# Attention scores of two heads on their own rows, expert down products half by half, and the last norm's gain ahead of its root

## The chip, the core and the metric

The kernel runs on one NeuronCore of a Trainium2 chip. The metric is the device time of one execution in microseconds (us), and less is better. The core has TensorE (PE in the profile; PEld is its weight load), VectorE (DVE), ScalarE (ACT), GpSimd (POOL) and SyncE (SP), which issues the transfers.

## What is computed

The reference is a transformer in float32 for one sequence of 256 tokens of 1024 channels. First come two layers, each a gated feed-forward block, a mixer and a second feed-forward block. Then come a state-space and short-convolution layer, a mixture of 16 experts of which each token uses two, and a last norm.

A mixer has three kinds of attention side by side, and a projection joins them:

```python
o_a = mla_mixer(h_a, ...)    # 6 heads, keys of 96
o_b = nsa_mixer(h_b, ...)    # 6 heads of 64 in 2 key groups: compressed + selected + window
o_c = diff_mixer(h_c, ...)   # 4 heads, each the difference of two softmaxes, keys of 32
x = x + jnp.concatenate([o_a, o_b, o_c], axis=-1) @ w_out[l]
```

The experts and the end are

```python
for e in range(N_EXPERTS):
    h = jax.nn.silu(t @ w_gate[e]) * (t @ w_up[e])
    out = out + combine[:, e:e + 1] * (h @ w_down[e])
...
return rmsnorm_2(h, norm_final)[:, N_META:]
```

## The kernel before, in words

The program is written with tiles and pools. A scheduler puts the instructions of each engine in order by its own estimate of when each can run, with the order of the program as the first guide. `in_turns` issues a first product and binds the others to come after it. `behind` does the same for any instructions.

Large weights are loaded by SP into tiles `st` (four buffers), 1 MB each, and split into a high and a low part (`wh`, `wl`: ScalarE at L166, VectorE at L167), which enter as separate products.

TensorE's products all bear the line of the helper `mm` (L98), and many copies on ScalarE that of a helper too, so they are told apart by their tiles.

In a mixer the string `ORDER` (L40) gives the order of the steps. A `w` step is a group of input columns, `mp`, `np` and `dp` prepare the three kinds of attention, `m0` to `m5`, `n0` to `n5` and `d0` to `d3` are heads, and `df` ends the differential ones. PSUM has eight banks here: three with tag S (scores, and half of the output projection's results), two with T (transposes), one with O (outputs of a pair of heads) and two with W (input columns, the differential outputs `po`, and the other half of the projection). A bank is free for the next user when its last reader is done.

A head goes like this. `scores` (L744; `nsa_head` has its own for the compressed and selected branch) makes a bank S of scores for the second and first half of the queries against the keys, and adds the causal mask as a product with the identity. `softmax` takes maxima on VectorE (L725), exponentials with their sums on ScalarE (L729) and reciprocals on VectorE (L732). For the compressed branch it also clamps (L727, L731). The gates follow at L734. `scale_rows` scales the weights on POOL or VectorE (L739). Then come three transposes (`ptp`, L691), a copy to `PT` and the products with the values. These wait in a list until two heads are there, and `pv_pair` does both in turns, each into its own half of the partitions of one bank (`opair`). `store_o` splits the result into `oh` and `ol`.

An nsa query tile holds a head of key group 0 on rows 0 to 63 and a head of group 1 on rows 64 to 127. The keys `ks` and `kw` (L802, L803) are stored once for each group, with zeros in the other group's rows, so that a product over all 128 rows gives the scores of one head. The differential keys `kC` (L892) are stored four times in the same way, each with 32 rows filled by a copy at L905. POOL fills in the zeros (L804, L805, L894). Heads of a pair are `n0` and `n1`, `n2` and `n3`, `n4` and `n5`. With `divmod(h, 3)` the head's number gives the group and the query tile.

The output projection (from L973) loads four units of `w_out` with one transfer each and goes over the chunks of `oh` and `ol` in the order 0, 1, 3, 4, 5, 6, 7, 2. Its products run wherever TensorE has time.

The experts run in eight rounds of two experts with 64 slots each. A round makes gate and up products, their activation (L1786 to L1788), transposes (L1800, copied at L1802), the down products into two banks `y0` and `y1` for the halves of the channels (L1803 on), their scaled high and low parts `ys` (L1634, L1814), and, one round later, `add`, which sums them into four banks `acc[t][half]` for two token tiles and two halves. The weights come in pieces of 512 KB into a ring of 44 places. `finish` (L1818 on) takes sums of squares of the four banks, the inverse root (`moe_inv`, L1570 on), and multiplies by root and gain into `os`, which leaves in four transfers.

## Time and profile before

| | us |
|---|---|
| median of three runs (lowest, highest) | 1529.91 (1529.6, 1532.09) |
| the profiled execution | 1532.0 |
| its span, first to last instruction | 1529.8 |
| TensorE busy in the span | 1492.0 |
| VectorE busy | 1025.1 |
| ScalarE busy | 729.7 |

The mean granted TensorE clock was 0.994 of full speed. The profile is of one execution, and the durations in the text are from that one. A row of a timeline begins with the start in us from the span's beginning, then the length of the merged instructions, the engine, the line, the operation and what is written from what. Successive instructions of an engine overlap by some tens of nanoseconds, so that a length is a little more than an engine's step.

### The profile page before, as it was taken

Reading aid. Unit: us, or ns where it says so; the run is one execution under the profiler, and the core shown is the slowest. Engines: PE = TensorE matmul, PEld = TensorE weight load, DVE = VectorE, ACT = ScalarE, POOL = GpSimd, SP = SyncE. Lnnn points to the kernel's source line nnn. Section 1 sums busy time; section 2 is a strip of 40 time slices with the busy share of each in tenths; the row PEclk is TensorE's granted clock in tenths of the full one; section 3 lists DMA queues with packets and bytes.
Section 4 is the critical chain, followed back from the end, with each engine's and each line's share of the span. In section 5 each row is a group of like instructions: output and inputs, shape, how many; then the busy total and the mean of one; then the engine's idle time right before and its main releaser. Section 6 shows DMA issues by size and latency. Waiting matters only on the chain.

```text
span 1529.8 us, 25415 instructions
## 1 busy us (share of the span) xinstructions
PE 1492.0 (98%) x9970; PEld 1253.6 (82%) x9970; DVE 1025.1 (67%) x2013; ACT 729.7 (48%) x1382; POOL 91.4 (6%) x142
## 2 busy tenths in 40 slices
PE   8999999999999999999999999999899999999996
PEld 7999998788999989999888999999799987344432
DVE  6886775868677786778576877779988875122112
ACT  6555565755454555455665655547554442011011
POOL 0000000520000000000025000000510100000000
PEclk9999999999999999999999999999999999999999
DMA  7756664216555565655640555566533588999993
GB/s 252 246 175 193 189 164 145 78 56 205 186 188 193 167 193 192 193 192 164 169 130 2 193 185 176 192 192 207 153 123 116 189 296 336 359 393 393 393 394 117
DMA packets 223559, 308.93 MB, mean 202 GB/s; under 512 B 20908, under 2 KB 167608, under 8 KB 223432
## 3 DMA queue, kind: packets, MB, share of 16 engines
q1 hardware_dynamic: 223128, 306.71, 60.1%
q8 instruction: 80, 1.31, 0.4%
q10 hardware_dynamic: 304, 0.53, 0.1%
q14 instruction: 47, 0.39, 0.1%
HBM read 306.16 MB, written 1.05 MB: 201 GB/s over the span
## 4 chain that ended last, share of the span: by engine, by line
PE 92%; DVE 5%; ACT 1%; issue 1%; DMA 0%; POOL 0%; ACTq 0%; DVEq 0%
PE gu L98 32%; PE acc L98 16%; PE proj L98 6%; PE win L98 6%; PE gate L98 4%; PE y L98 4%; PE up L98 4%; PE h L98 3%; PE wo L98 3%; PE S L98 3%; PE moe L98 1%; PE opair L98 1%; PE ptp L691 1%; PE zp L98 1%; PE xgp L98 1%; DVE wl L167 1%
## 5 line engine op out<-in xcount | busy, mean ns | idle before, releaser
L167 DVE TENSOR_TENSOR wl<-st,wh 128x1024 fp32r<-128x1024 f32 (+1 forms) x370 | 447.5, 1220 | 198.9 <-ACT wh L166 187.7
L166 ACT ACTIVATE wh<-st 128x1024 fp32r<-128x1024 f32 (+1 forms) x382 | 399.3, 1059 | 336.5 <-PE gu L98 134.4
L98 PE MATMUL gu<-xhl,wh 128*128 128x512 f32 (+1 forms) x1440 | 487.8, 392 | 3.1 <-ACT wh L166 2.2
L98 PE MATMUL gu<-xhl,wl 128*128 128x256 f32 x1408 | 381.6, 280 | 0.0
L98 PEld LDWEIGHTS gu<-xhl,wh 128*128 128x128 f32 x1440 | 268.2, 190 | 61.0 <-ACT wh L166 2.6
L98 PEld LDWEIGHTS gu<-xhl,wl 128*128 128x128 f32 x1408 | 260.8, 189 | 0.3
L98 PE MATMUL acc<-hx,wh 128*128 128x256 f32 x1408 | 252.1, 281 | 0.0
L98 PEld LDWEIGHTS acc<-hx,wh 128*128 128x128 f32 x1408 | 216.3, 188 | 1.6
L98 PE MATMUL acc<-hx,wl 128*128 128x256 f32 x704 | 196.8, 281 | 0.0
L98 PE MATMUL proj<-uhl,wh 128*128 128x272 f32 (+2 forms) x592 | 127.6, 306 | 5.3 <-DVE dv L1184 1.6
L98 PEld LDWEIGHTS acc<-hx,wl 128*128 128x128 f32 x704 | 132.6, 188 | 0.0
L98 PE MATMUL win<-wh,xhl 128*128 128x256 f32 (+1 forms) x576 | 109.7, 286 | 0.2 <-DVE xT L410 0.2
L98 PEld LDWEIGHTS proj<-uhl,wh 128*128 128x128 f32 x592 | 95.9, 191 | 10.5 <-ACT cv L1222 2.8
L98 PE MATMUL proj<-uhl,wl 128*128 128x272 f32 (+2 forms) x328 | 95.0, 290 | 0.0
L98 PEld LDWEIGHTS win<-wh,xhl 128*128 128x128 f32 x576 | 90.8, 191 | 4.2 <-issue 3.4
L98 PE MATMUL win<-wl,xhl 128*128 128x256 f32 (+1 forms) x288 | 81.9, 284 | 0.0
L394 ACT ACTIVATE hx<-up 128x512 fp32r<-128x512 f32 x44 | 27.7, 630 | 87.8 <-DVE up L393 87.8
L98 PEld LDWEIGHTS proj<-uhl,wl 128*128 128x128 f32 x328 | 62.5, 191 | 0.2
L1814 DVE SCALAR_TENSOR_TENSOR ys<-y,rc,ys 128x512 fp32r<-128x512 f32 x16 | 11.7, 749 | 67.2 <-ACT ys L1634 66.8
L739 POOL TENSOR_SCALAR P<-P,mx 128x128 f32<-128x128 f32 (+2 forms) x88 | 53.2, 621 | 57.9 <-DVE mx L732 41.8
L729 ACT ACTIVATE P<-S,mx 128x256 f32<-128x256 f32 (+2 forms) x128 | 48.9, 394 | 13.4 <-DVE mx L725 3.6
L98 PEld LDWEIGHTS win<-wl,xhl 128*128 128x128 f32 x288 | 55.0, 191 | 0.3
(522 smaller groups left out, 2133.7 us busy)
## 6 DMA issues: line engine op xcount, KB each, us to landing
st<-ffn_wg SPq DMA_DIRECT2D x44, 1024.0 KB, 5.7
st<-ffn_wu SPq DMA_DIRECT2D x44, 1024.0 KB, 5.4
st<-ffn_wd SPq DMA_DIRECT2D x44, 1024.0 KB, 4.7
st<-w_in SPq DMA_DIRECT2D x36, 1024.0 KB, 5.4
st<-w_out SPq DMA_DIRECT2D x16, 1024.0 KB
mf<-expert_w_gate SPq DMA_DIRECT2D x25, 512.0 KB, 9.8
mf<-expert_w_down SPq DMA_DIRECT2D x21, 512.0 KB, 10.7
mf<-expert_w_up SPq DMA_DIRECT2D x18, 512.0 KB, 11.3
```

Source lines behind the costliest of these rows:

```text
L98: return self.nc.tensor.matmul(out, lhsT, rhs, start=start, stop=stop, skip_group_check=True)
L166: hi = self.nc.scalar.activation(hl[0], src, AF.Copy)
L167: sub = (self.nc.gpsimd if lo[i] == "p" else self.nc.vector).tensor_sub(hl[1], src, hl[0].bitcast(F32))
L394: nc.scalar.activation(hh, up, AF.Copy)
L691: tr(p[:, i * 128:(i + 1) * 128], b, ident)
L729: nc.scalar.activation(P[:, d], s[:, c], AF.Exp, bias=m[:, 0, i:i + 1], accum_out=m[:, 1, i:i + 1])
L739: (nc.gpsimd if key + str(i) in "c0 c1 c2 d0 d1 m0 w0 w1".split() else nc.vector).tensor_scalar(P[:, d], P[:, d], r[:, i:i + 1], None, op0 ...
L1814: V.scalar_tensor_tensor(yl, py[half], rc[:, 1:2], yh.bitcast(F32), op0=OP.mult, op1=OP.subtract)
```

## The change

The change has four parts.

1. Scores. `ks`, `kw` and `kC` are stored once, without zeros. The new `scores_pair`, and the same by hand in `nsa_pair`, computes two heads in turns, each with the rows of the query tile that are its own (64 for nsa, 32 for the differential heads) into a bank S of its own. The masks are added on all rows afterwards. `nsa_pair(hg)` takes the heads hg and 3 + hg of one query tile together, and `ORDER` names the pairs. MLA heads stay as they were.
2. Output weights. As the pairs are now other heads, their rows of `w_out` are loaded in another order, by four transfers a unit in place of one.
3. Experts. The down products finish the first half of the channels and then the second, where they alternated. `add` goes through the halves likewise.
4. Last norm. The gain is multiplied into the first halves before the root is known, and ScalarE then scales them in place. VectorE does the second halves in one step each. All four sums of squares are on ScalarE, where one was on VectorE.

```diff
@@ L40 @@
-ORDER = "w01 w5 w2 mp m0 m1 w8 w3 w4 w6 np w7 dp m2 m3 d0 d1 n0 n1 d2 d3 n2 n3 n4 n5 m4 df m5"
+ORDER = "w01 w5 w2 mp m0 m1 w8 w3 w4 w6 np w7 dp m2 m3 d0 d1 n0 d2 d3 n1 n2 m4 df m5"
...
+        def scores_pair(banks, q, k, rows):
+
+            in_turns([lambda s=s, r=r, c=c, t=t, n=n: self.mm(s[:, c], q[t][r], k[r, 0:n], t == 1, False)
+                      for t, c, n in ((1, C1, 256), (0, C0, 128)) for s, r in zip(banks, rows)])
+            for s in banks:
+                self.mm(s[:, 128:256], self.identb, self.maskb, False, False)
+                self.mm(s[:, C0], self.identb, self.maskb, False, True)
...
-            ks = ap.tile([128, 2, 16 + T], F32, name="ks", tag="hA")
-            kw = ap.tile([128, 2, T], F32, name="kw", tag="cqT")
-            nc.gpsimd.memset(ks, 0.0)
-            nc.gpsimd.memset(kw, 0.0)
+            ks = ap.tile([128, 16 + T], F32, name="ks", tag="hA")
+            kw = ap.tile([128, T], F32, name="kw", tag="cqT")
+            nc.gpsimd.memset(ks[:, 15:16], 0.0)
...
-            for g in range(2):
-                q = slice(g * 64, (g + 1) * 64)
-                nc.vector.tensor_copy(ks[q, g, 16:16 + T], p3[q, 0:256])
-                nc.vector.tensor_copy(kw[q, g], p3[q, 256:512])
+            nc.vector.tensor_copy(ks[:, 16:16 + T], p3[:, 0:256])
+            nc.vector.tensor_copy(kw, p3[:, 256:512])
...
-            for g in range(2):
-                ACT(ks[g * 64:(g + 1) * 64, g, 0:15], p[g * 64:(g + 1) * 64, 0:15], scale=0.5)
+            ACT(ks[:, 0:15], p[:, 0:15], scale=0.5)
...
-        def nsa_head(h):
...
-            s = self.bank("S", "S")
-            self.mm(s[:, 0:272], qt[1], ks[:, g], True, False)
-            self.mm(s[:, 0:16], im, self.cmask[:, 1], False, False)
-            self.mm(s[:, 144:272], im, mb, False, False)
-            self.mm(s[:, 272:416], qt[0], ks[:, g, 0:144], False, False)
-            self.mm(s[:, 272:288], im, self.cmask[:, 0], False, False)
-            self.mm(s[:, 288:416], im, mb, False, True)
...
-            s = self.bank("S", "S")
-            scores(s, qt, kw[:, g], kw[:, g, 0:128])
...
+        def nsa_pair(hg):
+
+            rows = [slice(64, 128), slice(0, 64)]
+
+            two = [self.bank("S", "S") for _ in range(2)]
+            in_turns([lambda s=s, r=r, t=t, c=c, n=n: self.mm(s[:, c:c + n], qt[t][r], ks[r, 0:n], t == 1, False)
+                      for t, c, n in ((1, 0, 272), (0, 272, 144)) for s, r in zip(two[::-1], rows)])
+            for s in two:
+                self.mm(s[:, 0:16], im, self.cmask[:, 1], False, False)
+                self.mm(s[:, 144:272], im, mb, False, False)
+                self.mm(s[:, 272:288], im, self.cmask[:, 0], False, False)
+                self.mm(s[:, 288:416], im, mb, False, True)
+            for g, s in enumerate(two):
+                h = 3 * g + hg
+                P = ap.tile([128, 416], F32, name="P", tag="P", bufs=6)
+                scale_rows(P, SEGC, softmax(s, P, SEGC, gt[:, h, 0:4], -1e29), "c")
+                p, pt, n = transposes(blocks(P), "ptp")
+                nc.scalar.copy(pt, p[:, 0:n])
+                p2 = self.bank("T", "ptc")
+                cpt = ap.tile([16, T], F32, name="cpt", tag="cpt", bufs=2)
+                for t in range(2):
+                    tr(p2[0:16, t * 128:(t + 1) * 128], P[:, 384 + t * 16:400 + t * 16], ident)
+                nc.vector.tensor_copy(cpt, p2[0:16, 0:T])
+                pv("s", pt, [hV[:, t, 128 + g * 64:192 + g * 64] for t in range(2)])
+                waiting.setdefault("c", []).append((cpt, vcmp[0:15, g * 64:(g + 1) * 64]))
+            o = self.bank("O", "opair")
+            pv_pair(o, "s", True, False)
+            c0, c1 = waiting.pop("c")
+            in_turns([lambda o_=o_, c=c: self.mm(o_, c[1], c[0][0:15], False, False)
+                      for o_, c in ((o[64:128, 0:256], c1), (o[0:64, 0:256], c0))])
+            two = [self.bank("S", "S") for _ in range(2)]
+            scores_pair(two[::-1], qt, kw, rows)
+            for g, s in enumerate(two):
+                P = ap.tile([128, 384], F32, name="P", tag="P", bufs=6)
+                scale_rows(P, SEGS, softmax(s, P, SEGS, gt[:, 3 * g + hg, 4:6]), "w")
+                p, pt, n = transposes(blocks(P), "ptp")
+                nc.vector.tensor_copy(pt, p[:, 0:n])
+                pv("w", pt, [hV[:, t, 256 + g * 64:320 + g * 64] for t in range(2)])
+            pv_pair(o, "w", False, True)
+            store_o(3 + hg, o[:, 0:256])
...
-            kC = [ap.tile([128, 4, T], F32, name="kC", tag=tag) for tag in ("kC0", "hC")]
-            for k in kC:
-                nc.gpsimd.memset(k, 0.0)
+            kC = ap.tile([128, 2, T], F32, name="kC", tag="kC0")
...
-            for c in range(2):
-                for i in range(4):
-                    q = slice(i * 32, (i + 1) * 32)
-                    (nc.vector.tensor_copy if i % 2 else nc.scalar.copy)(kC[c][q, i], p2[q, c * T:(c + 1) * T])
+            nc.vector.tensor_copy(kC, p2[:].rearrange("p (c t) -> p c t", c=2))
...
-            for j in range(2):
-                k = kC[c][:, 2 * (h % 2) + j]
-                s = self.bank("S", "S")
-                scores(s, halves(qC[:, c]), k, k[:, 0:128])
+            two = [self.bank("S", "S") for _ in range(2)]
+            r0 = h % 2 * 64
+            scores_pair(two[::-1], halves(qC[:, c]), kC[:, c], [slice(r0 + 32, r0 + 64), slice(r0, r0 + 32)])
+            for s in two:
...
-        wo = [self.cols(a["w_out"][l], (b * 256, b * 256 + 256)) for b in range(4)]
+
+        def wo_unit(b):
+
+            st = self.wp.tile([128, 2048], F32, name="st", tag="st", bufs=4)
+            v = st[:].rearrange("p (k n) -> p k n", n=256)
+            w = a["w_out"][l][:, b * 256:(b + 1) * 256]
+            rows = lambda r, n, p: w[r:r + n, :].rearrange("(k p) c -> p k c", p=p)
+            nc.sync.dma_start(v[:, 0:3], rows(0, 384, 128))
+            for g in range(2):
+                nc.sync.dma_start(v[g * 64:(g + 1) * 64, 3:6], rows(384 + g * 192, 192, 64))
+            self.loaded = nc.sync.dma_start(v[:, 6:8], rows(768, 256, 128)).ins
+            return st, KD, 256
+
+        wo = [wo_unit(b) for b in range(4)]
         for b in range(4):
             for j, (wh, wl) in enumerate(self.split(wo[b], "n")):
...
-                for t in range(2):
-                    for half in range(2):
+                for half in range(2):
+                    for t in range(2):
...
-                for k in range(4):
-                    for half in range(2):
+                for half in range(2):
+                    for k in range(4):
...
-            V.tensor_copy(ht_, acc[1][0])
-            V.scalar_tensor_tensor(th_, ht_, 1.0, acc[1][0], op0=OP.mult, op1=OP.mult, accum_out=ss[:, 1:2])
-            for t, half in ((0, 0), (0, 1), (1, 1)):
-                self.moe_sumsq(t, half, os[:, t, half])
+
+            for t in range(2):
+                self.moe_sumsq(t, 0, os[:, t, 1])
+                V.tensor_mul(os[:, t, 0], acc[t][0], gB[:, 0:512])
+            for t in range(2):
+                self.moe_sumsq(t, 1, (th_, ht_)[t])
             for t in range(2):
                 self.moe_inv(t)
+                ACT(os[:, t, 0], os[:, t, 0], scale=r[:, t:t + 1])
+                V.scalar_tensor_tensor(os[:, t, 1], acc[t][1], r[:, t:t + 1], gB[:, 512:1024], op0=OP.mult, op1=OP.mult)
                 for half in range(2):
-                    o = os[:, t, half]
                     c = slice(half * 512, (half + 1) * 512)
-                    if half:
-                        ACT(o, acc[t][half], scale=r[:, t:t + 1])
-                        (V if t else nc.gpsimd).tensor_mul(o, o, gB[:, c])
-                    else:
-                        V.scalar_tensor_tensor(o, acc[t][half], r[:, t:t + 1], gB[:, c], op0=OP.mult, op1=OP.mult)
-                    (nc.scalar if half else nc.sync).dma_start(self.out[0, t * 128:(t + 1) * 128, c], o)
+                    (nc.sync if half else nc.scalar).dma_start(self.out[0, t * 128:(t + 1) * 128, c], os[:, t, half])
 
         round_(units, S, xg, True)
         finish()
```

## Rows read from the trace of the kernel before

**Rows 1.** The page: busy time by engine, and the chain by engine.

```profile
PE 1492.0 (98%) x9970; PEld 1253.6 (82%) x9970; DVE 1025.1 (67%) x2013; ACT 729.7 (48%) x1382; POOL 91.4 (6%) x142
...
PE 92%; DVE 5%; ACT 1%; issue 1%; DMA 0%; POOL 0%; ACTq 0%; DVEq 0%
```

**Rows 2.** Windows, first mixer: length, busy us (x) by engine, PEclk, DMA share, GB/s.

```profile
276.00:310.00 34.00, 33.06 (x258) 26.82 (x257) 31.15 (x137) 27.00 (x124) 21.95 (x36) 1.00 0.15 48
310.00:342.00 32.00, 32.00 (x268) 28.30 (x266) 19.81 (x50) 15.08 (x31) 4.95 (x8) 1.00 0.14 41
```

**Rows 3.** Timeline of PE, 282 to 285.9 us: start, us, what, shapes, count.

```profile
282.90 0.22 PE L98 MATMUL S<-maskb,identb 128*128 128x128 bf16 x1
283.05 0.87 PE L98 MATMUL opair<-PT,vm 128*64 128x256 f32 x8
283.85 0.73 PE L98 MATMUL S<-ks,qT 128*128 128x272 f32 x2
...
284.88 0.65 PE L98 MATMUL S<-kw,qT 128*128 128x256 f32 x2
...
285.75 0.39 PE L691 MATMUL ptp<-ident,P 128*128 128x128 f32 x2
```

**Rows 4.** Timeline of all engines, 277.3 to 278.6 us; in brackets idle time and releaser.

```profile
277.83 0.46 ACT L729 ACTIVATE P<-S,mx 128x256 f32<-128x256 f32 x1
277.87 0.62 DVE L725 TENSOR_REDUCE mx<-S 128x1 f32<-128x128 f32 x2
...
278.44 0.48 PE L98 MATMUL S<-kC,qC 128*128 128x256 f32 x1 [0.85 <-ACT P L729]
...
278.59 0.37 ACT L729 ACTIVATE P<-S,mx 128x128 f32<-128x128 f32 x1
```

**Rows 5.** Timeline of DVE, 286.5 to 290.6 us, a compressed head.

```profile
286.59 0.17 DVE L727 TENSOR_SCALAR mx<-mx 128x4 f32<-128x4 f32 x1
...
287.31 0.78 DVE L725 TENSOR_REDUCE mx<-S 128x1 f32<-128x16 f32 x4
```

**Rows 6.** Timeline of ACT, the same stretch and head.

```profile
286.85 0.27 ACT L729 ACTIVATE P<-S,mx 128x16 f32<-128x16 f32 x1
...
287.70 0.48 ACT L729 ACTIVATE P<-S,mx 128x256 f32<-128x256 f32 x1
```

**Rows 7.** Tile S, 276 to 310 us: ns min/median/max, first and last start.

```profile
L98 PE MATMUL S<-KT,QT x14: 275/377/433, 275.7 to 309.9; 96*128 96x256 f32 x8, 96*128 96x128 f32 x6
```

**Rows 8.** Windows of tile wo alone: PE, PEld and DVE busy us (x).

```profile
276.00:310.00 34.00, 1.81 (x9) 1.27 (x9) 0.00 (x0) 1.00 0.15 48
```

**Rows 9.** Timeline of DVE, 272.5 to 278 us.

```profile
273.10 0.42 DVE L819 COPY ks<-ktb 64x256 f32<-64x256 f32 x1
...
274.66 0.19 DVE L798 SCALAR_TENSOR_TENSOR h<-h,h 64x30 f32<-64x30 f32 x1
276.31 0.42 DVE L905 COPY kC<-kct 32x256 f32<-32x256 f32 x1 [1.47 <-ACT kC L905]
```

**Rows 10.** Timeline of SP's issues, 225 to 345 us.

```profile
238.32 20.70 SPq L150 DMA_DIRECT2D st<-w_out  x4
265.31 0.37 SPq L150 DMA_DIRECT2D st<-ffn_wg  x1
```

**Rows 11.** The chain that ended last, 1500 to 1530 us: start, us, what.

```profile
1508.28 7.18 PE y L98 x32
...
1515.49 0.70 ACT ys L1634
...
1517.81 1.85 ACT os L1567 x6
...
1521.89 1.41 DVE os L1836 x2
1523.30 1.20 DVE os L1834
```

**Rows 12.** Windows, late experts: columns as in rows 2.

```profile
1500.00:1510.00 10.00, 8.92 (x42) 3.01 (x39) 1.80 (x3) 0.78 (x2) 0.00 (x0) 1.00 0.03 11
```

More of the change, by code (lines that the diff above doesn't have):

```diff
@@ L968, in _mixer @@
             else:
-                {"m": mla_head, "n": nsa_head, "d": diff_head}[step[0]](int(step[1]))
+                {"m": mla_head, "n": nsa_pair, "d": diff_head}[step[0]](int(step[1]))
         KO = [int(c) for c in "01345672"]
-        wo = [self.cols(a["w_out"][l], (b * 256, b * 256 + 256)) for b in range(4)]
+        def wo_unit(b):
[9 more added lines that the diff above has]
+        wo = [wo_unit(b) for b in range(4)]
         for b in range(4):
@@ L1768, in add @@
             def add(q, ST, ys):
-                for t in range(2):
-                    for half in range(2):
+                for half in range(2):
+                    for t in range(2):
                         for i in range(2):
```

27 lines of the change are left out of this document (removed).

## The prediction

> **What bounds the kernel now.** I read the page first. Its part 1 has TensorE busy for 98% of the span, and the chain that ended last runs on TensorE for 92% of it [rows 1]. So work taken from TensorE counts, unless another wait replaces it. The page is an average, so I then cut the span where the diff acts: two mixers (a little over 4% of the span each, counted from the first attention score to the end of the output projection), and the experts with the final norm.
>
> The windows split the first mixer at 310 us, just after its last score. From 276 to 310 TensorE is busy for 33.06 of 34 us, but VectorE is too, for 31.15, and ScalarE for 27.00. From 310 to 342 TensorE is busy all 32 us and VectorE for 19.81 [rows 2]. So the first stretch has two engines near their limit, the second one only. The second mixer runs the same steps.
>
> Third, the timeline of one score and of what frees its PSUM bank. Scores go into three banks (tag S). At 278.44 TensorE had been idle for 0.85 us, and the row names ScalarE's exponential P at L729 as the releaser: the bank was not free before that was read [rows 4]. The three banks are therefore a limit already, if a small one.
>
> **The scores: what TensorE saves.** Before, a window head takes from 284.88 to 285.75, 0.87 us, and a compressed one from 283.85 to 284.88, 1.03 us [rows 3]. Each does its passes on 128 rows, most of them zeros. After, two heads use half the rows each (a quarter, for the differential heads), in turns. The trace has no such row halves, but it has column halves in turns: the pair of value products `opair`, eight passes of the same widths, takes 0.80 us from 283.05 to 283.85, with the change back to the whole array in it [rows 3]. Going in costs 0.10 us (the mask at 282.90 to 283.05, 0.15 us, against 0.05 from the last mask to the transposes at 285.75). With two masks of 0.05 a pair of window or differential heads is 0.10 + 0.80 + 0.10 = 1.0 us, against 1.74. A compressed pair has 32 columns more (0.05 us) and masks of 0.08 four times: 1.27 against 2.06. Three window, four differential and three compressed pairs a layer save 7 x 0.74 + 3 x 0.79 = 7.5 us of TensorE. That is one end. The other is that row halves don't overlap: a pair is then 2 x 0.77 of passes + 0.20 of changes + 0.10 of masks = 1.84 us, 0.1 worse than now. I take the overlap, as `opair` is the nearest row.
>
> **The scores: what they add.** A pair holds two banks of the three, and the next pair needs two. So pair follows pair at the time for which the first head of a pair holds its bank, where before a third score could begin while two were still being read. That time, with nothing queued: the second mask begins 0.85 us after the first pass and its result is read 0.27 us later (0.22, the mask row [rows 3], and an estimated 0.05 to VectorE), 1.12. The two maxima begin at 277.87 and the exponentials at 278.59, 0.72. The exponentials take 0.37 + 0.46, 0.83. From the end of the last (278.29) to the next score at 278.44 is 0.15. Together 2.82 us [rows 4]. For a compressed pair: 1.25 to the first maximum, 0.78 for four maxima, 0.26 from the clamp to the exponentials, 1.33 for four of those (286.85 to 288.18), 0.15: 3.77 us [rows 5, 6]. Ten pairs: 7 x 2.82 + 3 x 3.77 = 31.1 us. The first pair waits for the bank of m2, as the score at 278.44 does now, 2.7 us after the first score. So the last score of all (m5) comes 33.8 us after the first, if nothing ever queues. Before, the scores last from 275.7 to 309.9, 34.2 us [rows 7]. The saving of 7.5 us is gone at that point even without a queue.
>
> And there is one. Now 24 scores go through three banks in 34.2 us, so a bank is held for 3 x 34.2 / 24 = 4.3 us. By the sums above, with 0.82 us to the last mask of a single head and 0.97 for a compressed one, the hold with nothing queued is 2.8 and 3.8 us, 3.0 on average. So 1.3 us of each hold is waiting, mostly for VectorE, which is busy for 92% of the stretch [rows 2]. After the change, such waiting lengthens every period: between 0 and 13 us for ten pairs. I take 0.5 us a pair, 5.0 us: heads in flight fall from three to about 2.4, so the queues are shorter, but VectorE still has nearly all of its work and must do it in the same time.
>
> The Trainium skill, TensorEngine Tiling (Array Packing), Restrictions and Gotchas, warns of this: row tiles write to different PSUM banks, so row tiling raises the pressure on PSUM. No row of the trace shows row tiles; the 0.85 us at 278.44 shows the pressure.
>
> What of it reaches the end? The idle time could be filled with output projection, which has no bank for that: before the last score it gets 1.81 us, in the one W bank that the differential output leaves [rows 8]. I allow three more of its products, 0.4 us. The 32 us of TensorE work behind the last score stay [rows 2].
>
> **The preparation.** Four copies of keys (L819, L820) stand on VectorE between 273.10 and 274.66, ahead of the step at L798 that the next TensorE products read [rows 9]. Two full ones replace them: 0.8 us less. The eight copies into kC (0.42 us each on VectorE [rows 9]) become one of 128x512, estimated at 0.7 us from the width; they stood among the maxima, and I count them in the lighter queue. The zero fills on POOL go; POOL was busy 21.95 of 34 us, so nothing [rows 2].
>
> Per layer: 33.8 - 34.2 + 5.0 - 0.4 - 0.8 = +3.4 us, and +6.8 for both.
>
> **The output weights.** Each of the four units is loaded by four transfers instead of one, half of them on 64 partitions. All four are issued between 238.32 and 259.0 us, and such an issue is 0.37 us of SP [rows 10]: 12 more are 4.4 us of SP's time, and halved speed for the two short ones would add under 2 us to a landing. Behind them on SP stand the next stage's weights, the first issued at 265.31, six microseconds later [rows 10], and the bulk of the projection runs after 310 us [rows 2, 8]. I cost it at nothing; without that cover it would be those 2 us once a layer.
>
> **The experts and the end.** Down products by half leave TensorE's count as it is. Weights of the down product are held up to half of 7.18 us longer [rows 11], which could hold up loads; but from 1500 us on DMA is at 0.03, so the last weights are there 8 us before the product at 1508.28 that reads them [rows 11, 12]. Nothing. At the end it pays: the first half's ScalarE step (0.70 us) and the VectorE step behind it run under the second half's products. So the last sums come some 0.7 us earlier, and the squares, which ran from 1517.81 to 1519.66, end some 0.8 earlier, at 1518.85. The root (1519.66 to 1521.89, 2.2 us) stays. Behind it stood two steps of 0.70 and a product of 1.20, 2.61 us; after, VectorE has the two of 0.70 alone, beside two of ScalarE: 1.4, so 1.2 less [rows 11]. Sum 2.0 us; at least 1.2 (the second step alone), at most 3.0.
>
> **Sum.** +6.8 - 2.0 = +4.8 us. The profiled execution took 1532.0 us for a span of 1529.8; the median of the runs, 1529.91, lies 2.1 us under it. On the median that is 1534.7 us, and about 1537 beside a profile.
>
> **Rivals.** *The cycle is not queued* (23%). If maxima and exponentials of a pair are served at once, a layer has 33.8 - 34.2 - 0.4 - 0.8 = -1.6 us, the total -3.2 - 2.0: 1525 us. For it: VectorE loses copies and fewer heads compete. Against: it would have to be busy for 92% of the time with no wait. *TensorE's saving comes through* (10%): 7.5 + 0.8 us a layer and the 2.0, 1511 us. That would be so if the order found other work for the third bank's time. The Trainium skill, TensorEngine Tiling (Array Packing), Overview, gives up to 2x for a contraction of 64 or less, and it points to this case. Against it stands the bank sum. *The halves don't overlap* (7%): each period grows by 0.8 us, 8 us a layer, 1551 us. *It cancels* (12%): around 1530. The forecast itself (48%) spans 1529 to 1545, from 0.2 to 1.0 us of waiting a pair. It decides at 0.26 us of waiting a pair, where 2 x (2.6 - 1.6) - 2.0 is nothing.
>
> **The numbers.** A measurement can tell about 0.2%, 3 us. Faster holds the two first rivals, less a little: 0.32. Same: the cancelling case and the low end of the forecast, 0.20. Slower: 0.48. The range, 1519 to 1546, leaves out the full saving and the missing overlap.
>
> **What would show it.** Right: in the first mixer, gaps of TensorE ahead of S that ScalarE's P at L729 ends, ten a layer, with TensorE well under 33 of 34 us; pairs of scores in some 1.0 us; the last score 37 us or more after the first; the end from the last down product to the last output 2 us shorter. Wrong: scores over in under 33 us; or TensorE full with output projection moved ahead of 310 us; or pairs of 1.8 us.

## The result, and the profile after

The changed kernel takes **1564.4 us** (median of four, 1564.34 to 1564.71) against 1529.88 before, a ratio of 1.0221 (95%: 1.0208 to 1.0234). That is 34.5 us slower, where 4.8 were forecast with 1546 as the end of the range.

The page of the kernel after, in its lines for busy time and granted clock [rows 1]:

```profile
PE 1525.1 (98%) x9970; PEld 1271.4 (81%) x9970; DVE 1020.3 (65%) x2001; ACT 726.6 (47%) x1374; POOL 84.7 (5%) x135
...
PEclk9999999589999999999998999999999999999998
```

TensorE has as many instructions as before (9970) and is busy for 33.1 us longer. The clock row has a 5 in its eighth slice (273 to 313 us, the first mixer). The windows of after, of the first mixer and then of the second (columns as in [rows 2]):

```profile
276.00:310.00 34.00, 34.00 (x143) 24.15 (x140) 16.19 (x69) 15.47 (x69) 11.98 (x20) 0.55 0.15 48
310.00:342.00 32.00, 31.63 (x205) 24.14 (x205) 19.98 (x91) 13.90 (x64) 13.33 (x24) 0.83 0.00 1
```

```profile
829.00:843.00 14.00, 14.00 (x62) 8.82 (x62) 6.41 (x26) 3.57 (x18) 3.76 (x5) 0.51 0.00 0
```

From 276 to 310 us TensorE is busy all 34 us, and does 143 instructions where it did 258. VectorE falls from 31.15 to 16.19 us. So TensorE is the bound, but not through more work: the granted clock is 0.55. In the clock's records of the trace it stands at 1.2 GHz for 41.0 us on end, from 279.7 to 320.7, and for 13.7 us in the second mixer, from 829.2. Before, it stood at 2.4 GHz through both mixers. With TensorE full, 54.6 us at half speed lose at most half, 27.3 us. That can be the larger part of the 34.5, and the prediction has no word of it.

The timeline of PE of after, where three scores of differential heads follow one another at 2.4 GHz [rows 3]:

```profile
276.44 0.22 PE L98 MATMUL S<-maskb,identb 128*128 128x128 bf16 x1
276.59 0.92 PE L98 MATMUL S<-kC,qC 32*128 32x256 f32 x4
277.44 0.28 PE L98 MATMUL S<-maskb,identb 128*128 128x128 bf16 x2
277.65 0.92 PE L98 MATMUL S<-kC,qC 32*128 32x256 f32 x4
278.50 0.28 PE L98 MATMUL S<-maskb,identb 128*128 128x128 bf16 x2
278.71 0.92 PE L98 MATMUL S<-kC,qC 32*128 32x256 f32 x4
```

This looks like pairs of 1.06 us, as forecast. It isn't. One product is two records here (before, a head's 256 columns are x2 [rows 3]), so x4 and two masks are *one head*: the differential scores are 32 records a layer in both kernels, for the eight scores of four heads with two softmaxes each. (In what follows such a score is called a head, and a head that has only its own 32 or 64 rows is called narrow.) The scheduler put the second product of the leading head ahead of the other head's first. **No pair is in turns**: the 80 records of nsa and differential scores in the first mixer come as two wide and two short ones, head by head, and so do those of the second. A narrow head on 32 rows takes 1.06 us (277.65 to 278.71) where one on 128 rows took 0.87.

The other places. The last MLA score before and after, and the projection of after, in the views of their tiles. (The window of [rows 7] ends at 310 us and misses the last two records of before.)

```profile
L98 PE MATMUL S<-KT,QT x16: 275/352/433, 275.7 to 310.3; 96*128 96x256 f32 x8, 96*128 96x128 f32 x8
```

```profile
L98 PE MATMUL S<-KT,QT x12: 275/352/432, 275.6 to 334.7; 96*128 96x256 f32 x6, 96*128 96x128 f32 x6
```

```profile
L98 PE MATMUL wo<-ohl,wl x64: 278/283/415, 292.8 to 363.1; 128*128 128x256 f32 x64
```

The last score starts at 334.7 instead of 310.3, the last product of the projection at 363.1 instead of 342.0. DVE ahead of the attention [rows 9], and SP's issues of the output weights [rows 10]:

```profile
272.94 0.42 DVE L824 COPY ks<-ktb 128x256 f32<-128x256 f32 x1
273.28 0.41 DVE L825 COPY kw<-ktb 128x256 f32<-128x256 f32 x1
273.73 0.19 DVE L806 SCALAR_TENSOR_TENSOR h<-h,h 64x30 f32<-64x30 f32 x1
274.99 0.69 DVE L904 COPY kC<-kct 128x512 f32<-128x512 f32 x1 [1.07 <-PE kct L902]
```

```profile
238.24 0.37 SPq L979 DMA_DIRECT2D st<-w_out  x1
238.66 1.32 SPq L981 DMA_DIRECT2D st<-w_out  x2
240.02 0.60 SPq L982 DMA_DIRECT2D st<-w_out  x1
...
265.23 0.37 SPq L150 DMA_DIRECT2D st<-ffn_wg  x1
```

The end, in the chain that ended last [rows 11]:

```profile
1540.03 7.18 PE y L98 x32
...
1547.23 0.70 ACT ys L1646
...
1547.97 2.25 PE moe L98 x8
...
1550.24 0.58 ACT os L1579 x2
1550.82 1.17 ACT acts L1579 x4
...
1555.20 0.72 ACT os L1646
```

ScalarE's first step on `ys` starts behind all 32 down products, as before. So the first half isn't done any sooner: here too the new order did not come through, as products that still alternate between the halves would have it. The four squares, all on ScalarE, end 4.8 us behind the down products (1551.99), where before it was 4.2. From the end of the down products to the last output's issue it is 8.75 us (1555.95), 9.1 before (1524.53). From there to the end of the span it is 6.65 us where it was 5.3, so the end as a whole is 1.0 us longer, not 2.0 shorter. The issues of before on ScalarE's queue, the last two:

```profile
1523.98 0.89 ACTq L1837 DMA_DIRECT2D out<-os  x2
```

### The profile page after: what moved, and what is told of

The parts are those of the page before. It is cut to its first block, busy times and chain, and to the rows that moved or that the text cites. A ratio compares the mean times of both kernels' runs of the same rounds, so it can differ in the third digit from the quotient of the medians.

```text
span 1562.6 us, 25417 instructions
## 1 busy us (share of the span) xinstructions
PE 1525.1 (98%) x9970; PEld 1271.4 (81%) x9970; DVE 1020.3 (65%) x2001; ACT 726.6 (47%) x1374; POOL 84.7 (5%) x135
## 4 chain that ended last, share of the span: by engine, by line
PE 93%; DVE 4%; ACT 2%; issue 1%; DMA 0%; ACTq 0%; DVEq 0%
PE gu L98 32%; PE acc L98 16%; PE proj L98 7%; PE win L98 6%; PE S L98 4%; PE gate L98 4%; PE y L98 4%; PE up L98 4%; PE h L98 3%; PE wo L98 3%; PE moe L98 1%; PE opair L98 1%; PE ptp L691 1%; PE zp L98 1%; PE xgp L98 1%; DVE wl L167 1%
## 5 line engine op out<-in xcount | busy, mean ns | idle before, releaser
L729 ACT ACTIVATE P<-S,mx 128x128 f32<-128x128 f32 (+2 forms) x128 | 49.0, 398 | 29.4 <-DVE mx L725 21.2
L739 POOL TENSOR_SCALAR P<-P,mx 128x128 f32<-128x128 f32 (+1 forms) x88 | 53.6, 635 | 143.8 <-DVE mx L732 94.9
```

What stands on the lines that cost most here:

```text
L729: nc.scalar.activation(P[:, d], s[:, c], AF.Exp, bias=m[:, 0, i:i + 1], accum_out=m[:, 1, i:i + 1])
L739: (nc.gpsimd if key + str(i) in "c0 c1 c2 d0 d1 m0 w0 w1".split() else nc.vector).tensor_scalar(P[:, d], P[:, d], r[:, i:i + 1], None, op0 ...
```

## The experiments

Ratios are to the kernel before on the same chip, with 95% intervals.

### Which part costs what

**The mixer of before, with the experts and norm of after.**

> The mixer is that of before; experts and last norm are those of after. Theory: the 34.5 us are all the mixer's, so this kernel takes 1529.9 to 1531.5 us (the end took 14.3 us from the last down product before and 15.4 after, and 0.6 us came between the gate and the last sum), and the granted clock has no stretch at 1.2 GHz between 276 and 320 us. Rival: the experts' new order costs several us that the shift of the trace hid; then over 1535 us. The recorded forecast would have 1527.9 us here.

1531.34 us, ratio 1.0001 (0.9992 to 1.001). The whole loss is the mixers'. The experts and the end bring neither gain nor loss.

**Full rows in the differential pairs, in all pairs, in the nsa pairs.** Zero-padded keys return, pairs and order stay:

```diff
-scores_pair(two[::-1], halves(qC[:, c]), kC[:, c], [slice(r0 + 32, r0 + 64), slice(r0, r0 + 32)])
+scores_pair(two[::-1], halves(qC[:, c]), [kC[c][:, i0 + 1], kC[c][:, i0]], [slice(0, 128)] * 2)
```

> As after, pairs and order kept, but the four differential pairs of a layer use zero-padded keys on all 128 rows; the nsa pairs stay on 64 rows. Theory: the products on 32 rows are what the clock fell behind, 41.0 us of 1.2 GHz in the first mixer and 13.7 us in the second, of which at most half is lost, 27.3 us; without them the clock stays at 2.4 GHz through both mixers and the time is 1537 to 1543 us (1564.4 - 27.3, and up to 3 us a layer of longer products). Rival one: the clock falls because pairs wait for banks, whatever the rows; then it falls here too and the time stays over 1558 us. Rival two: 64 rows alone bring it down as well; then a stretch at 1.2 GHz begins behind a pair of window or compressed heads.

> As after, pairs and order kept, but every pair uses zero-padded keys on all 128 rows, so no product works on its own rows. Theory: the clock stays at 2.4 GHz in both mixers; the time is that of the bank cycle and of TensorE's old work, 1537 to 1552 us (27.3 us less than after for the clock, up to 7.5 us a layer more for the products). Rival one (the bank cycle brings the clock down): the stretch at 1.2 GHz is here too, over 1560 us.

> As after, but the six nsa pairs of a layer use zero-padded keys on all 128 rows; the differential pairs stay on 32 rows. Theory: the clock falls behind the 32-row pairs as in after, some 40 us in the first mixer, and the time is 1560 to 1573 us. Rival two (64 rows bring the clock down): with those gone the stretches are shorter by half or more, and the time is under 1553 us.

1540.09 us (1.0059; 1.0043 to 1.0074), 1540.36 (1.0057; 1.0042 to 1.0073) and 1541.21 (1.007; 1.0055 to 1.0086). The windows from 276 to 310 us, of differential full, nsa full, and all full:

```profile
276.00:310.00 34.00, 31.93 (x231) 24.79 (x231) 27.30 (x118) 21.44 (x99) 16.49 (x28) 1.00 0.11 36
```

```profile
276.00:310.00 34.00, 32.66 (x242) 25.48 (x242) 27.51 (x122) 22.13 (x103) 17.43 (x29) 1.00 0.11 36
```

```profile
276.00:310.00 34.00, 31.24 (x239) 25.58 (x238) 28.08 (x120) 22.28 (x101) 16.91 (x28) 1.00 0.15 47
```

My theory said that the 32-row products bring the clock down. It fell with the third kernel, which has them all and keeps 2.4 GHz in the mixers of its trace. (That execution is the fastest of its four, 1537.07 us; the others are 1540.57 to 1541.95 at mean clocks down to 0.989.) With either kind of head on full rows the clock holds here, and the time is what was expected of after without its two stretches. With both kinds narrow it falls. And since the kernels with one kind narrow take no longer than the one with all rows full, the longer passes of narrow heads cost nothing there by themselves.

Full rows are no warrant, though. With all pairs on full rows the clock stands at 1.2 GHz for 6.8 us from 791.6, early in the second mixer's attention. With the mixer of before, in an execution of 1535.14 us, the longest of eleven, it does so for 10.2 us from 786.9. Both come right behind small products with some idle time of TensorE (busy for 2.57 of 3.6 us and 2.97 of 4). Before has the same there, 2.97 of 4, and keeps its clock.

**Full rows and the order of after, but one bank a head:**

```diff
-two = [self.bank("S", "S") for _ in range(2)]
-scores_pair(two[::-1], qt, [kw[:, 1], kw[:, 0]], rows)
-for g, s in enumerate(two):
+for g in range(2):
+    s = self.bank("S", "S")
+    scores(s, qt, kw[:, g], kw[:, g, 0:128])
```

> As the kernel with full rows in every pair, but each head takes one bank when its turn comes, with the mask behind each product as before; the order of the heads and the loads of the output weights are those of after. Theory: of its 9 us over before (1540.4), most is the pair that takes two banks of three at once, so this kernel takes 1531 to 1535 us. Rival: the order of the heads or the four transfers a unit cost it; then it stays at 1538 to 1542 us.

1531.31 us, 1.0001 (0.9992 to 1.001): that of before, with after's order of heads, output weights, experts and norm. So pairs on two banks by themselves cost 0.56%, 8.6 us. (The masks go back behind each product with that, too.) The same stretch of both in the windows, first the pairs and then one bank a head:

```profile
276.00:318.00 42.00, 38.69 (x295) 30.79 (x294) 35.76 (x156) 28.64 (x132) 21.39 (x36) 1.00 0.12 39
```

```profile
276.00:318.00 42.00, 41.06 (x325) 32.96 (x323) 37.06 (x163) 30.44 (x137) 27.25 (x44) 1.00 0.12 39
```

The view of tile S lists what the idle time ahead of it ended on (us, times); its line for the exponentials, again the pairs first:

```profile
  ACT P L729: 6.8, 12
```

```profile
  ACT P L729: 2.1, 3
```

With pairs, waiting for the exponentials is 6.8 us in 12 waits, where one bank a head has 2.1 in 3 (summed over matmuls and weight loads). That is the forecast's bank cycle. The last score of the pairs, in the same view:

```profile
L98 PE MATMUL S<-KT,QT x16: 274/352/433, 275.6 to 317.3; 96*128 96x256 f32 x8, 96*128 96x128 f32 x8
```

It comes 41.7 us after the first, where before it was 34.6.

### Pairs really in turns

In the first kernel each of the four products is bound behind the one before. In the second the masks come first, so that both banks are in hand ahead of the first product. In the third, built on the second, only the nsa pairs are in turns, and differential heads are single on full rows.

```diff
-        def in_turns(products):
+        def in_turns(products, strict=False):
...
-            with self.behind(lead.ins):
-                for product in products[1:]:
-                    product()
+            for product in products[1:]:
+                with self.behind(lead.ins):
+                    p = product()
+                if strict:
+                    lead = p
```

```diff
+in_turns([lambda s=s: self.mm(s[:, 128:256], self.identb, self.maskb, True, False) for s in banks]
+         + [lambda s=s: self.mm(s[:, C0], self.identb, self.maskb, False, False) for s in banks]
+         + [lambda s=s, r=r, c=c, t=t, n=n: self.mm(s[:, c], q[t][r], k[r, 0:n], False, t == 0)
+            for t, c, n in ((1, C1, 256), (0, C0, 128)) for s, r in zip(banks, rows)], True)
```

> As after, but each of a pair's four score products is issued behind the one before it. In the trace of after a pair's heads are not in turns: two passes of one head on 256 columns, two on 128, its masks, and only then the other head, and each such head takes 1.06 us at 2.4 GHz where the full rows took 0.87. Theory: that is why TensorE saved nothing and why it worked on a part of its rows for long stretches; with the products really in turns the row halves overlap, two heads take about 1.1 us, the clock stays at 2.4 GHz, and the time is 1530 to 1541 us. Rival one: row halves do not overlap on the chip; then two heads take about 1.7 to 2.1 us even in turns and the clock falls again, over 1555 us. Rival two: they overlap, but the lead waits on TensorE for the other head's bank, 0.5 to 1.5 us at most pairs; then 1540 to 1555 us.

> As after, but the masks are added first, in both banks, and then the four score products, each behind the one before it, so that both banks are free before the first and nothing stands between the four. Theory: four products of 256, 256, 128 and 128 columns take 0.75 to 0.9 us in all at 2.4 GHz, the clock stays there, and the time is 1530 to 1541 us. Rival one (no overlap of row halves): the four take 1.4 us or more.

> As the kernel with masks first and all pairs truly in turns, but the differential heads go singly on zero-padded keys with one bank each; only the nsa pairs, whose two halves fill 128 rows, are in turns. Three score banks. Theory: all rows are at work in every score, so the clock stays at 2.4 GHz; six bank-bound pairs a layer in place of ten leave a part of the 9 us: 1532 to 1538 us. Rival: a pair of 64-row halves in turns lets the clock fall like narrow heads do; over 1545 us.

1586.03 us (1.0369; 1.0353 to 1.0385), 1554.85 (1.0161; 1.0144 to 1.0179) and 1535.69 (1.003; 1.002 to 1.0039). In the first the clock is at 1.2 GHz for 51.2 and 64.9 us, and the time lies where its first rival put it (over 1555 us). But the halves do overlap, as the next kernel shows. What fails is that the lead goes ahead alone and the other three products wait for the other head's bank:

```profile
281.61 0.72 PE L98 MATMUL S<-ks,qT 64*128 64x272 f32 x2
...
283.42 1.41 PE L98 MATMUL S<-ks,qT 64*128 64x272 f32 x6 [0.83 <-ACT P L731]
```

The timeline of PE of the second:

```profile
276.17 0.33 PE L98 MATMUL S<-maskb,identb 128*128 128x128 bf16 x3 [0.78 <-ACT P L731]
276.43 0.92 PE L98 MATMUL S<-kC,qC 32*128 32x256 f32 x8
277.28 0.23 PE L98 MATMUL S<-maskb,identb 128*128 128x128 bf16 x1
277.35 0.50 PE L691 MATMUL ptp<-ident,P 128*128 128x128 f32 x3
...
279.23 0.33 PE L98 MATMUL S<-maskb,identb 128*128 128x128 bf16 x3 [0.57 <-ACT P L731]
279.49 0.92 PE L98 MATMUL S<-kC,qC 32*128 32x256 f32 x8
280.34 0.87 PE L98 MATMUL opair<-PT,vm 128*64 128x256 f32 x8
```

Now eight records, both heads, take 0.85 us (279.49 to 280.34). **Row halves do overlap**, and the forecast's price for the pair, 0.80 and the changes, was right. Its other term can be read here too: the first two pairs stand 3.06 us apart (276.17 to 279.23; forecast 2.82 and some queueing), and in this mixer TensorE waits for ScalarE's exponentials ahead of scores in five places, 2.9 us in all. The warning of the Trainium skill that row tiles press on PSUM (TensorEngine Tiling (Array Packing), Restrictions and Gotchas) is borne out by these waits. TensorE is busy for only 26.08 of the 34 us:

```profile
276.00:310.00 34.00, 26.08 (x204) 18.53 (x203) 24.08 (x99) 18.12 (x86) 15.55 (x26) 0.95 0.10 33
```

The clock fell here as well, in four stretches of 37.5 us together. The profiled execution (1555.60 us) is 24.8 us over the median of before, 1530.77. At most half of the 37.5, 18.8, is the clock's, so some 6 us have another cause; the waits name the banks, beside a forecast of 4.8. This split holds for that execution alone: the other three are at mean clocks of 0.977 and 0.981, below its 0.986. The third kernel keeps the clock, with all 128 rows at work in each pair, and lands in the range expected, 0.3% over before:

```profile
276.00:310.00 34.00, 29.09 (x240) 21.97 (x241) 29.16 (x128) 22.48 (x101) 18.39 (x30) 1.00 0.12 40
```

TensorE is busy 4 us less in this stretch than before (29.09 against 33.06 [rows 2]), and the kernel is not done sooner.

### Own rows without pairs, and the clock

Before, with keys stored once and each head on its own rows, singly: all heads, the nsa heads alone, the differential heads alone.

```diff
-scores(s, qt, kw[:, g], kw[:, g, 0:128])
+scores(s, [v[r] for v in qt], kw[r], kw[r, 0:128])
```

> As before (its order of heads, its output weights, its experts and norm), but the keys are stored once and every nsa and differential head uses its own 64 or 32 rows alone, one head and one bank at a time, nothing in turns. Theory: rows left unused are what the clock falls behind, with no pair needed, when both kinds of heads leave them unused: a stretch of 20 us or more at 1.2 GHz in the first mixer, 1540 to 1560 us. Rival one: the pairs are needed too (they let narrow heads stand next to each other); then no stretch in the mixers and 1527 to 1531 us (the preparation is 0.8 us a layer shorter).

> As before, but the nsa keys are stored once and each nsa head uses its own 64 rows, one head and one bank at a time; the differential heads stay on zero-padded keys. Theory: with half of the narrow work the clock holds, as it did with nsa pairs on 64 rows; TensorE's passes are as long as on 128 rows, and the two copies less ahead of the attention give 0.8 us a layer: 1528 to 1530.5 us. Rival: each head pays 0.1 to 0.2 us for going over to its rows and back, 12 a layer; then 1531 to 1535 us.

> As before, but the differential keys are stored once, copied in one step in place of eight, and each differential head uses its own 32 rows, one head and one bank at a time; the nsa heads stay on zero-padded keys. Theory: the clock holds, and VectorE and ScalarE lose 1 us or so of copies a layer; 1528 to 1531 us. Rival: each head pays 0.1 to 0.2 us for the change of rows, 8 a layer; then 1531 to 1534 us.

1600.31 us (1.0465; 1.044 to 1.049), 1554.26 (1.0142; 1.0088 to 1.0197) and 1552.03 (1.0135; 1.0118 to 1.0152). All three are beyond what was expected. In the first:

```profile
276.00:310.00 34.00, 34.00 (x115) 19.94 (x115) 14.65 (x63) 14.02 (x64) 11.27 (x18) 0.53 0.12 38
```

No pairs at all, TensorE busy without a break, and a clock of 1.2 GHz for 44.4 us, later for 64.9. So narrow heads are enough, and the pairs are not what brings the clock down. With one kind narrow it falls too, in shorter stretches (6.8 to 13.7 us), where pairs with one kind narrow kept it. Whether it is the rows left unused or the more frequent changes of rows, these kernels don't tell apart. Single narrow heads with the mask between two products cost more than the paired ones, which change rows once a head: 1.36 us a differential head (277.04 to 278.40 in the third), since a change of rows costs about 0.1 us: from a mask to the next narrow product it is 0.16 (277.67 to 277.83), on full rows 0.05.

```profile
277.04 0.69 PE L98 MATMUL S<-kC,qC 32*128 32x256 f32 x2
277.67 0.23 PE L98 MATMUL S<-maskb,identb 128*128 128x128 bf16 x1
277.83 0.48 PE L98 MATMUL S<-kC,qC 32*128 32x128 f32 x2
```

**More work for TensorE.** After, with four useless products a head on all rows:

```diff
 for s in banks:
+    for _ in range(4):
+        self.mm(s[:, 0:128], self.zw, self.identb, False, False)
     self.mm(s[:, 128:256], self.identb, self.maskb, False, False)
```

> As after, with four useless products a head added (zero weights on all 128 rows, 128 columns, 0.05 us each, 20 heads a layer: 4.3 us more of TensorE a layer; they add nothing to the scores). Theory: TensorE working on all rows more often keeps its clock up; if the stretches at 1.2 GHz go, the time falls to 1540 to 1552 us although TensorE has 8.6 us more to do. Rival: the clock falls all the same, then 1570 us or more.

1558.38 us (1.0169; 1.0118 to 1.0219), with four runs of 1547.37 to 1562.71. All four are under the lowest of after (1564.34), but the intervals still touch (after: 1.0208 to 1.0234), so a gain in time is likely and not shown, and it is less than was expected. What is clear is the clock: a mean of 0.982 to 0.994 in the four, against 0.975 and 0.976 in those of after. The stretches are 10.2 and 10.2 us here:

```profile
276.00:310.00 34.00, 33.35 (x239) 24.75 (x237) 20.92 (x85) 15.99 (x74) 13.09 (x20) 0.87 0.11 36
```

The run of 1547.37 had a mean granted clock of 0.994, that of before. After less 27.3 for the clock plus 8.6 of added work (160 products of 0.054 us) is 1545.7.

### Four score banks

S gets a fourth bank and W gives one up; input columns go to W and O by turns: before, all pairs in turns, nsa pairs in turns.

```diff
-        with self.phase(f"mixer{l}", **dict(S=3, T=2, O=1, W=2)):
+        with self.phase(f"mixer{l}", **dict(S=4, T=2, O=1, W=1)):
...
-            ps = [self.bank(tags.pop(0) if tags else "W", "win") for _ in ids]
+            ps = [self.bank(tags.pop(0) if tags else "WO"[(turn.append(1) or len(turn)) % 2], "win") for _ in ids]
```

> As before, with four score banks and one bank W, input columns on W and O by turns. Theory: before is held up by score banks only a little (0.85 us ahead of a head), so 1526 to 1530 us. Rival: giving up the second W costs 2 us a layer or more where the output projection filled TensorE; then 1533 to 1540 us.

> As the kernel with masks first and all pairs truly in turns (1554.9), but four score banks in place of three; the second bank W is given up, and groups of input columns go to W and to O by turns. Theory: that kernel's TensorE gaps ahead of pairs (0.57 to 1.14 us, ended by ScalarE's exponentials) are the bank cycle; with two pairs' worth of banks they go, TensorE keeps its 0.7 us a pair, and the clock, which fell where TensorE waited between narrow pairs, falls less: 1520 to 1540 us. Rival: the gaps come from VectorE and ScalarE being late whatever the banks, or one W bank costs as much ahead of the attention; then 1545 us or more.

> As the kernel with only the nsa pairs in turns, with four score banks and one bank W. Theory: the bank cycle goes and TensorE's saving on six pairs, 4 to 5 us a layer, comes through with the clock at 2.4 GHz: 1519 to 1528 us, below both kernels. Rival: VectorE, busy for 92% of the stretch, holds the scores back instead; then 1528 to 1534 us.

1572.43 us (1.0268), 1587.59 (1.0371) and 1571.32 (1.0272), slower than all that was expected but for the rival of the second, that one bank W costs as much ahead of the attention. They decide nothing about score banks: ahead of the attention TensorE now waits, busy for 21.25 of 28 us in the first (before 26.03), and the clock falls there, for 20.5 us from 278.0:

```profile
262.00:290.00 28.00, 21.25 (x141) 19.75 (x140) 13.29 (x33) 8.43 (x17) 0.53 (x1) 0.79 0.40 126
```

### The end

Built on the kernel with the mixer of before: the second half's down products behind the first half's last one, in all rounds, in the last round alone, and that with the norm of before.

```diff
 for half in range(2):
-    for k in range(4):
+    with self.behind(*last_ if q == 7 else []):
+        for k in range(4):
...
+    last_ = [y.ins]
```

> As the kernel with the mixer of before, but the second half's down products are issued behind the last one of the first half (in the trace of after they still alternate). Theory: now ScalarE's first step on ys runs under the second half's products, so from the last down product to the last output it is 0.7 to 1.5 us shorter than in the kernel with the mixer of before: 1529.5 to 1531 us beside its 1531.3, a difference within what can be measured. Rival: the last down products start later or wait, then no gain or a loss of 1 us or more over eight rounds.

> Mixer of before, experts and norm of after, and only in the last round the second half's down products are issued behind the first half's last one. Theory: with halves in all rounds the stretch from the end of the last down products to the last output's issue was 7.1 us, against 9.1 before and 8.7 after, while the rounds lost some 3 us; with the last round alone the rounds lose nothing and the end's 2 us come through: 1528.5 to 1530 us beside some 1531 of before. Rival: the 3 us are lost in the last rounds or at the end as well; then 1531 to 1534 us.

> As the kernel above, but with the last norm of before (one sum of squares on VectorE, gains multiplied in behind the root). Theory: the products' order brings 0.7 us and the norm's steps 1.2 us, so this one is some 1 us slower than the one above: 1529.5 to 1531 us. Rival: the norm's new steps bring nothing, since all four sums now stand behind one another on ScalarE; then the two are equal within 0.5 us.

1534.12 us (1.0019; 1.001 to 1.0028), 1530.03 (0.9992; 0.9983 to 1.0001) and 1530.26 (0.9993; 0.9984 to 1.0002). The chain of the second kernel:

```profile
1508.12 7.09 PE y L98 x32
1515.21 0.91 PE moe L98 x3
...
1516.14 0.70 ACT os L1567 x2
```

and ScalarE's timeline of it, where the first step now runs under the second half's products:

```profile
1511.90 0.69 ACT L1634 ACTIVATE ys<-y,rc 128x512 fp32r<-128x512 f32 x1 [3.83 <-PE y L98]
...
1522.34 0.37 ACTq L1838 DMA_DIRECT2D out<-os  x1
```

From the end of the down products (1515.21) to the last issue it is 7.13 us instead of 9.1: the forecast's 2.0, to a tenth. But the time from there to the end of the span grew from 5.3 to 6.75 us, so 1.4 of the 2.0 goes back. Here the last two outputs are issued together on both queues (1522.33 and 1522.34), where before all four came one by one from 1522.66 to 1524.53. With the norm of before, which issues the last one 0.55 us behind the others, the two stretches are 8.1 and 5.3. That the issues together are the reason is not shown. In all rounds the halves lose some 3 us: from the first gate product to the end of the last down product it is 220.0 us instead of 216.2. TensorE is busy 3.3 us longer with the same 1008 instructions. Of the products, gate and up are 1.9 and 1.3 us longer, the down products 0.7; why stays open. Neither of the two kernels with halves in the last round alone can be told from before, though the middle of both intervals lies under it.

## Why the prediction was wrong

The direction was right; the size was not, and the range didn't hold it. The step that failed is the price of TensorE's work. The prediction counts it in time at 2.4 GHz and puts the clock at nothing, without a reason; the runs show some 25 us in its place. Other kernels set this step apart. With pairs as they were compiled, one or both kinds of heads on full rows and the clock up, it takes 1540.09 to 1541.21 us, inside the range. With all pairs in turns, as forecast, and the clock down, it takes 1554.85, outside. That 1540 lies near the forecast of 1534.7 is in part luck: the pairs there are not in turns, and the 2.0 us of the end did not come. By its steps:

- *What TensorE saves, 7.5 us a layer.* This step failed too, but the sum doesn't use the 7.5: it took the bank cycle as the limit and from the pair only its 0.85 us of passes. It took "in turns" from the diff, and the compiled order has no pair in turns. The price itself held in the kernel that enforces the order, 0.85 us for eight passes. In after two heads of a pair take 2 x 1.06 us where they took 1.74, so a saving turned into 0.4 us more a pair. The rival "the halves don't overlap" (7%, 1551 us, 1.84 a pair) is what happened on TensorE, not because row halves can't overlap, but because they were never side by side.
- *What the banks add, 3.4 us a layer net.* The mechanism is shown: 8.6 us in all for pairs on full rows against one bank a head, with TensorE waiting for the exponentials at L729. The forecast had 6.8 for both layers. Its marks are there too: with pairs on full rows TensorE is busy for 31.24 of 34 us. Of its parts, the 32 us of TensorE work behind the last score did not stay: it is 28.4 in after (334.7 to 363.1) and with pairs on full rows, as fewer heads are still in flight by then (behind the last score `opair<-PT,hV` has 16 records, where it had 32). In return the last score comes 41.7 us after the first, where the sum had 38.8 (33.8 and 5.0 of queueing); before it was 34.6 and not 34.2, since the view that was read ended at 310 us. How much of it is queueing can't be read apart, as no kernel has all pairs in turns and a full clock.
- *The clock.* The prediction has no such step: up to 27.3 of the 34.5 us is lost to time at 1.2 GHz. Ahead of it stands the mean clock of before, 0.994 of full speed, and it asks nothing of what could change that.
- *The sign in the profile.* "TensorE well under 33 of 34 us" was named as the mark of the banks. In after it was 34.00 of 34, and the marks of the missing term were the clock column beside it and the count, 143 for 258.
- *Preparation, 0.8 us.* Right: from the first copy to the step at L798 (now L806) it is 0.79 us (272.94 to 273.73), where it was 1.56 (273.10 to 274.66 [rows 9]), and the copy into kC takes 0.69 us for an estimated 0.7.
- *Output weights, nothing.* Right: SP issues a unit in 2.4 us, the next stage's first weights go out at 265.23 (before 265.31 [rows 10]), and the kernel that has these loads with one bank a head is level with before.
- *Halves in the rounds, nothing.* True for after, where the order seems not to have changed; where it was bound, the rounds lost 3 us.
- *The end, 2.0 us.* Failed in after for the same reason, and the four squares on one engine end later as well: 0.3 us less to the last issue, 1.0 more to the end of the span. With the order enforced the 2.0 come at the last issue, and 0.5 of them at the end of the span.

The sum from the runs: nothing for order, weights, experts and end; 8.6 us for pairs on three banks; and 25.1 (0.0221 less 0.0057, of 1530) for both kinds of heads narrow, one after the other, which the stretches at 1.2 GHz are long enough to hold (27.3 at most). What stays open is what tips the clock: the kernel with nsa heads on full rows has the same three differential heads up to 279.5 us as after, in the same 1.06 us each, and its clock holds. And early in an attention it fell in kernels on full rows as well, for 6.8 and 10.2 us.

No kernel here beats the one before by more than can be measured. Before is the one to keep.

## What to carry to other kernels

Where a scheduler orders the instructions, an edit that writes products in turns or by halves is a wish: count the records of a group in the timeline against the products that it should hold before pricing what the order brings, and bind each product behind the last one if it matters. TensorE "busy" is time, not work: read the granted clock beside it and the number of instructions, above all after an edit that leaves rows of the array unused. And a pair that takes two buffers of three turns the pool into one buffer; ask for the cycle time of that pair before asking what it saves.

## What was unexpected of the hardware

The clock fell to 1.2 GHz while TensorE was busy without a gap, behind products on 32 and 64 rows, and stayed there for 41.0 us: 34.00 of 34 us busy at 0.55, and at 0.53 without any pairs. The Trainium skill, TensorE: Matmul & The Clock Gate, Part 1, says that the chip watches how busy TensorE has been and that activity releases the throttle. By the busy time of the profile these stretches should have run at 2.4 GHz; they differ from those that did in the rows in use and in the changes of rows. Its second failure mode in the same part, short idle times of TensorE between groups as PSUM banks are cycled, could fit the kernel with all pairs in turns (26.08 of 34 us busy, clock 0.95, then 0.84), though the one with only nsa pairs in turns waits too (29.09 of 34) at a clock of 1.00. It doesn't fit after, which has no such idle times.

Giving TensorE 8.6 us of useless products on all rows went with a higher mean clock in all four runs than in those of after, and all four were shorter. And where the clock is on edge, a kernel no longer has one time: nsa heads alone on their own rows took 1542.6 to 1560.0 us in four runs, with mean granted clocks of 0.994 and 0.982 at the two ends, while before stays within 5 us on the same chips.
